# The beginning of a two-layer backbone kernel: stationary modulation weights, loads in a fixed order, modulation work held back, two norms interleaved

## The chip, the cores and the metric

The kernel runs on one core of one Trainium2 chip. The time is device microseconds (us) of one execution, the median of several runs. Engines: PE (TensorE; its weight loads are PEld), DVE (VectorE), ACT (ScalarE), POOL (GpSimd) and SP (SyncE, whose queue issues all the DMAs here). Each engine executes its own instructions in a fixed order.

## The reference

Two layers run on 1024 latent and 128 context tokens, with the same weights. Each layer is modulated by a conditioning vector, one for each group of tokens:

```python
def modulation(cond, w, b):
    m = jax.nn.silu(cond) @ w + b
    return [t[:, None, :] for t in jnp.split(m, N_MOD, axis=-1)]   # shift1, scale1, gate1, shift2, scale2, gate2

def adaln(x, g, shift, scale):
    return rms_norm(x, g) * (1.0 + scale) + shift

for l in range(DEPTH):                      # DEPTH = 2, D_MODEL = 1024
    m_ctx = modulation(c_ctx[None, :], w_mod[l], b_mod[l])
    m_lat = modulation(c, w_mod[l], b_mod[l])
    h_ctx = adaln(ctx, g_norm_mix[l], m_ctx[0], m_ctx[1])
    h_lat = adaln(lat, g_norm_mix[l], m_lat[0], m_lat[1])
    # even l: latent attention and gated MLP from h;  odd l: convolution and pooling from h
    ctx = ctx + m_ctx[2] * mix_ctx
    lat = lat + m_lat[2] * mix_lat
    # then x = x + gate2 * ConvFFN(adaln(x, ..., shift2, scale2))
```

Before anything else of layer 0 can be multiplied, `h` is needed, and for it two of the six parts ("chunks") of the first modulation: chunk 1 (scale1) and chunk 0 (shift1), each a product of a 2 x 1024 operand (two conditioning vectors) with 1024 x 1024 weights of 4 MB.

## The kernel before

Activations are held transposed: 128 channels on the partitions, 8 channel tiles (`k`, KT = 8), 1154 token columns in three blocks of 384, 384 and 386 (`BLK`). Products of the layers are made of three float32r products each (high and low halves, `mm3`), while the modulation, the transposes and the sums of squares are plain float32. In the profile a float32 product is two records, a float32r product one.

A scheduler orders each engine's instructions from the program's order and priorities; `issue_after` and `follow` add an order that it must keep. What it decides is shown further down.

The beginning of `even()` (layer 0) goes like this. `load_x(0)` loads block 0 of the input. `norm_blk` gives four steps for a block: `add(k)` squares a channel tile (ACT) and adds it up (tile `nsum`), `chain` turns the sum into the reciprocal root (tile `st` by PE, `ms` by DVE, `rs` by POOL, the diagonal `dg` by DVE, `rb` by PE), `scaled` multiplies x by it and by the scale (DVE, in place), and `shifted` adds the shift and splits the result into high (ACT, L87) and low (DVE, L88) halves of `h`. `mod_pe` makes one modulation chunk on PE: for each `k` a load of 128 x 1024 weights (`mraw`, 512 KB, from a pool of RB = 8 buffers), and two products with the two-column operand `self.sc` as the stationary side and 512 weight columns as the moving side. The two rows that result are copied (`mrow`), transposed in eight small products (`mpt`), and the bias is added (`mod`).

`even_kv` then multiplies `h` of each block by two weights: per block three tiles of 128 tokens by `wB` (`kvps`, L652 to L654, 72 records) and one product by `wA` (`qps`, L76 to L78, 24 records). `wB` comes in three units (loads `raw<-in_evB_dram`) and `wA` in one (`in_evA_dram`), each split into halves by ACT and DVE (L66, L67). After the three blocks, ten groups (`expand`) make keys and values (`kvu`, L708 to L710) from transposed, split columns (`tp` by PE, `ckvT` by ACT and DVE).

The other chunks of layer 0's modulation that are needed early (`EARLY`, chunks 2, 4 and 3) are made on DVE, by `mod_dve_steps`: 48 steps, each a load of 128 x 512 weights (256 KB, two buffers) and two instructions that accumulate into `macc` (L154 for the first step of a half, else L157). They are taken one by one from the list `self.fill` at fixed places of the program (`drip`), two per `expand`, with a lower priority, so the scheduler may also put them earlier, where it holds DVE to be idle.

`FASTB` names the blocks whose sum of squares is added up on DVE alone; for the others POOL adds pairs.

Of the kernel before, what the change touches and what calls it, by code (L numbers as in the profile page):

```python
# [19 lines left out]
P = 128  # L20
# [23 lines left out]
class Net:  # L44
# [8 lines left out]

    def unit(self, src, n=1024, gain=None, pool=None):

        nc = self.nc
        raw = self.wraw.tile([P, 1024], F32, tag="raw", name=self.nm("raw"))
        nc.sync.dma_start(out=raw[:, :n], in_=src)
# [21 lines left out]
    def split(self, hi, lo, src, shift=None):  # L80
        nc = self.nc
        if shift is None:
            ins = nc.scalar.activation(hi, src, AF.Copy)  # L83
            nc.vector.tensor_tensor(out=lo, in0=src, in1=hi.bitcast(F32), op=ALU.subtract)  # L84
            return ins
        else:
            nc.scalar.activation(hi, src, AF.Identity, bias=shift)  # L87
            nc.vector.scalar_tensor_tensor(out=lo, in0=src, scalar=shift, in1=hi.bitcast(F32),  # L88
                                           op0=ALU.add, op1=ALU.subtract)


# [25 lines left out]

    def mod_pe(self, l, ch, pool, tag, rpool):

        nc = self.nc  # L120
        ps = [self.gp.tile([P, 512], F32, tag="gp", name=self.nm("mps")) for _ in range(2)]
        for k in range(KT):
            raw = rpool.tile([P, 1024], F32, tag="mraw", name=self.nm("mraw"))
            last = nc.sync.dma_start(out=raw, in_=self.ap["wmod"][l, k * P:(k + 1) * P, ch * D:(ch + 1) * D])
            for j in range(2):
                nc.tensor.matmul(ps[j][:2, :], self.sc[:, k, :], raw[:, j * 512:(j + 1) * 512],  # L126
                                 start=(k == 0), stop=(k == KT - 1))
        pt = self.sm.tile([P, 512], F32, tag="sm", name=self.nm("mpt"))
        for j in range(2):
            row = pool.tile([2, 512], F32, tag=tag, name=self.nm("mrow"))  # L130
            nc.vector.tensor_copy(row, ps[j][:2, :])
            for m in range(4):
                i = 2 * (j * 4 + m)
                nc.tensor.transpose(pt[:, i:i + 2], row[:, m * P:(m + 1) * P], self.ident[:2, :2])
        nc.vector.tensor_tensor(
            out=self.mod[l][:, ch * 8:(ch + 1) * 8, :], in0=pt[:, :16].rearrange("p (m c) -> p m c", c=2),
            in1=self.bmod[:, l, ch * 8:(ch + 1) * 8].unsqueeze(2).to_broadcast([P, 8, 2]), op=ALU.add)
        return last

    def mod_dve_steps(self, l, ch, pool, folded):  # L140
# [4 lines left out]
        def step(h, k):  # L145
            raw = pool.tile([P, 512], F32, tag=f"mraw{k % 2}", name=self.nm("mraw"))
            c0 = ch * D + h * 512
            nc.sync.dma_start(out=raw, in_=self.ap["wmod"][l, k * P:(k + 1) * P, c0:c0 + 512])
            if k == 0:
                acc[h] = pool.tile([P, 2, 512], F32, tag=f"macc{h if folded else 0}", name=self.nm("macc"))  # L150
            a = acc[h]
            for c in range(2):
                if k == 0:
                    nc.vector.tensor_scalar(out=a[:, c, :], in0=raw, scalar1=self.sc[:, k, c:c + 1], scalar2=None,  # L154
                                            op0=ALU.mult)
                else:
                    nc.vector.scalar_tensor_tensor(out=a[:, c, :], in0=raw, scalar=self.sc[:, k, c:c + 1],  # L157
                                                   in1=a[:, c, :], op0=ALU.mult, op1=ALU.add)
# [132 lines left out]
    def norm_blk(self, x, l, w, b, hb, pool, big=None, inplace=False):  # L291
# [25 lines left out]
        def shift(src, k, o, m, c):  # L317
            so = 0 if w == 0 else 24
            self.split(hb[:, 0, k, o:o + m], hb[:, 1, k, o:o + m], src, self.mod[l][:, so + k, c:c + 1])

# [6 lines left out]

        def scaled():
            for k in range(KT):
# [3 lines left out]
        def shifted():  # L333
            for k in range(KT):
                for (o, m, ro, c) in segs:
                    shift(x[:, k, c0 + o:c0 + o + m], k, o, m, c)

# [121 lines left out]
    def even(self):  # L459
# [5 lines left out]
        with ExitStack() as e1:  # L465
            hb = self.new_hb()
            with ExitStack() as e0:
                npool = e0.enter_context(tc.tile_pool(name="en", bufs=2, reuse_waits="tile"))
                rpool = e0.enter_context(tc.tile_pool(name="er", bufs=RB, reuse_waits="tile"))
                x0 = self.xpool.tile([P, KT, T], F32, tag="x", name="x0")  # L470

                def load_x(b):
                    c0, n = BLK[b]
                    nc.sync.dma_start(out=x0[:, :, c0:c0 + n], in_=ap["xt"][:, :, c0:c0 + n])
# [12 lines left out]
                last = self.mod_pe(0, 0, npool, "mrow", rpool)  # L487
                shifted()
                with tc.issue_after(last.ins):
                    load_x(1)  # L490
                    load_x(2)
                for b in (1, 2):
                    add, chain, scaled, shifted = norm(b)
                    for k in range(KT):
                        add(k)
                    chain()
                    scaled()
                    shifted()
# [118 lines left out]

    def even_kv(self, hb, kd, vd, cw, w1, w2, w3):

# [17 lines left out]

        wB = [self.unit(ap["evB"][:, s * 288:(s + n) * 288], n * 288) for s, n in ((0, 3), (3, 3), (6, 2))]
        wA = self.unit(ap["evA"][0])
        qc0 = c1.tile([P, 2, T], F32R, name="qc0")  # L640
# [636 lines left out]
    def run(self):  # L1277
        nc, tc, ap = self.nc, self.tc, self.ap
        self.open, self.fill = {}, []
        with ExitStack() as es:  # L1280
# [62 lines left out]
NS = 3  # L1343
FASTB = (1, 2)
PRF2 = 60
# [106 lines left out]
```

## Time and profile before

| what | value |
|---|---|
| time, median of 3 runs | 2801.76 us (2801.47 to 2802.89) |
| the profiled execution | 2798.91 us, its span 2797.1 us |
| PE busy | 2702.6 us, 97% of the span |
| DVE, ACT, POOL busy | 1889.4, 1010.8 and 375.6 us |
| first 45 us: PE busy, DMA | 32.58 us, 360 GB/s |
| 45 to 75 us: PE busy, DMA, mean granted TensorE clock | 21.83 us, 105 GB/s, 0.79 |

Each row of a timeline has the start, the length, the engine, the line, the operation, output<-inputs, the shapes and a count of merged instructions, and behind them how long the engine was idle and what ended that. A row of a table by stretch has the stretch, its length, busy time (and number of records) of PE, PEld, DVE, ACT and POOL, the granted TensorE clock (1.00 is full, 0.50 half), the DMA engines' busy share and the GB/s that they moved.

### The profile page before, as it was taken

The numbers are of one execution on the slowest core, as the hardware profiler recorded it, in microseconds if no ns is written. First come the engines' busy times: TensorE is split into PE (matmuls) and PEld (weight loads), VectorE is DVE, ScalarE is ACT, GpSimd is POOL, SyncE is SP. The second block draws the span as 40 slices with busy tenths as digits, with TensorE's granted clock in tenths as the row PEclk, the third lists the DMA queues.
The fourth block names the chain that finished last, engine by engine and source line by source line (L and its number), as shares of the span: only waits on it lengthen the run. The fifth ranks groups of instructions, "written<-read, shape, count | busy, mean of one in ns | idle before, by whom it ended". The sixth has DMA issues, their size and how long they took to land.

```text
span 2797.1 us, 38522 instructions
## 1 busy us (share of the span) xinstructions
PE 2702.6 (97%) x15444; PEld 2622.6 (94%) x15444; DVE 1889.4 (68%) x3120; ACT 1010.8 (36%) x1798; POOL 375.6 (13%) x433
## 2 busy tenths in 40 slices
PE   7999989999999999999999999989999999999999
PEld 3897978889999999999999999888999999999999
DVE  5873799998787788855453878887555455554445
ACT  3543278882343222222223331225422222222331
POOL 2354155540200010000000200002000000000000
PEclk9999999999999999999999999999999999999999
DMA  7254210007143444311111011011011111111111
GB/s 277 71 154 112 86 32 23 25 1 234 53 128 114 131 133 128 119 48 46 38 46 38 10 46 39 27 39 38 31 38 46 38 46 39 45 37 40 46 46 68
DMA packets 92851, 192.64 MB, mean 69 GB/s; under 512 B 9472, under 2 KB 43136, under 8 KB 92672
## 3 DMA queue, kind: packets, MB, share of 16 engines
q1 hardware_dynamic: 92672, 190.18, 21.3%
q8 instruction: 122, 2.00, 0.3%
q14 instruction: 57, 0.47, 0.1%
HBM read 170.20 MB, written 19.95 MB: 68 GB/s over the span
## 4 chain that ended last, share of the span: by engine, by line
PE 83%; DVE 10%; DMA 3%; ACT 2%; issue 1%; POOL 1%; SPq 0%; DVEq 0%; POOLq 0%; ACTq 0%
PE fps L76 13%; PE fps L77 13%; PE fps L78 13%; PE ops L76 8%; PE ops L78 8%; PE ops L77 8%; PE av L982 2%; DMA mraw<-in_wmod_dram 2%; PE ptp L971 1%; DVE macc L157 1%; PE ips L76 1%; PE ips L77 1%; PE ips L78 1%; PE Sa L995 1%; PE mps L126 1%
## 5 line engine op out<-in xcount | busy, mean ns | idle before, releaser
L76 PE MATMUL fps<-h,wt 128*128 128x384 f32 (+1 forms) x2112 | 711.8, 339 | 1.6 <-ACT z L401 1.2
L77 PE MATMUL fps<-h,wt 128*128 128x384 f32 (+1 forms) x2112 | 713.0, 338 | 0.0
L78 PE MATMUL fps<-h,wt 128*128 128x384 f32 (+1 forms) x2112 | 712.7, 338 | 0.0
L379 DVE SCALAR_TENSOR_TENSOR x<-ops,mod,x 128x384 f32<-128x384 f32 (+1 forms) x832 | 395.6, 513 | 235.3 <-PE ops L78 233.8
L67 DVE TENSOR_TENSOR wt<-raw,wt 128x1024 fp32r<-128x1024 f32 (+2 forms) x177 | 216.8, 1235 | 385.1 <-ACT wt L66 384.6
L77 PEld LDWEIGHTS fps<-h,wt 128*128 128x128 f32 x2112 | 398.6, 189 | 0.3
L76 PEld LDWEIGHTS fps<-h,wt 128*128 128x128 f32 x2112 | 396.2, 188 | 2.5 <-ACT z L401 1.5
L78 PEld LDWEIGHTS fps<-h,wt 128*128 128x128 f32 x2112 | 398.1, 189 | 0.0
L78 PE MATMUL ops<-act,wt 128*128 128x384 f32 (+1 forms) x1056 | 358.2, 339 | 0.0
L77 PE MATMUL ops<-act,wt 128*128 128x384 f32 (+1 forms) x1056 | 357.0, 338 | 0.0
L76 PE MATMUL ops<-act,wt 128*128 128x384 f32 (+1 forms) x1056 | 355.4, 339 | 0.0
L401 ACT ACTIVATE z<-fps 128x384 f32<-128x384 f32 (+1 forms) x264 | 129.0, 493 | 602.9 <-PE fps L78 602.6
L66 ACT ACTIVATE wt<-raw 128x1024 fp32r<-128x1024 f32 (+2 forms) x177 | 182.8, 1047 | 440.1 <-PE ops L78 316.2
L157 DVE SCALAR_TENSOR_TENSOR macc<-mraw,sc,macc 128x512 f32<-128x512 f32 x280 | 214.5, 796 | 42.1 <-DMA mraw<-in_wmod_dram 41.7
L76 PEld LDWEIGHTS ops<-act,wt 128*128 128x128 f32 x1056 | 199.6, 189 | 0.0
L77 PEld LDWEIGHTS ops<-act,wt 128*128 128x128 f32 x1056 | 198.7, 188 | 0.0
L78 PEld LDWEIGHTS ops<-act,wt 128*128 128x128 f32 x1056 | 198.6, 188 | 0.1
L1181 DVE SCALAR_TENSOR_TENSOR co<-cv,c_odw,co 128x1168 f32<-128x1168 f32 x92 | 133.2, 1451 | 19.1 <-ACT co L1174 18.2
L76 PE MATMUL ops<-h,wt 128*128 128x384 f32 (+1 forms) x384 | 132.7, 351 | 7.0 <-ACT h L83 5.4
L83 ACT ACTIVATE act<-c 128x1154 fp32r<-128x1154 f32 x44 | 51.5, 1171 | 227.9 <-DVE c L422 183.5
L77 PE MATMUL ops<-h,wt 128*128 128x384 f32 (+1 forms) x384 | 132.2, 344 | 0.9 <-DVE h L84 0.9
L410 DVE SCALAR_TENSOR_TENSOR c<-z,fdw,c 128x1153 f32<-128x1153 f32 x88 | 125.7, 1429 | 8.6 <-ACT c L408 7.7
(275 smaller groups left out, 4578.0 us busy)
## 6 DMA issues: line engine op xcount, KB each, us to landing
raw<-in_fin_dram SPq DMA_DIRECT2D x88, 512.0 KB, 3.6
mraw<-in_wmod_dram SPq DMA_DIRECT2D x160, 256.0 KB, 2.8
raw<-in_fout_dram SPq DMA_DIRECT2D x44, 512.0 KB, 3.5
mraw<-in_wmod_dram SPq DMA_DIRECT2D x16, 512.0 KB, 8.8
fold<-macc SPq DMA_DIRECT2D x14, 512.0 KB, 2.9
macc<-fold SPq DMA_DIRECT2D x56, 128.0 KB, 3.3
x<-in_xt_dram SPq DMA_DIRECT2D x4, 1536.0 KB, 10.3
raw<-in_odin_dram SPq DMA_DIRECT2D x12, 512.0 KB, 3.5
```

The source lines that it names most:

```text
L66: nc.scalar.activation(wt[:, 0, :n], raw[:, :n], AF.Copy)
L67: nc.vector.tensor_tensor(out=wt[:, 1, :n], in0=raw[:, :n], in1=wt[:, 0, :n].bitcast(F32), op=ALU.subtract)
L76: mm(out, wh, ah, start=start, stop=False)
L77: mm(out, wh, al, start=False, stop=False)
L78: mm(out, wl, ah, start=False, stop=stop)
L83: ins = nc.scalar.activation(hi, src, AF.Copy)
L157: nc.vector.scalar_tensor_tensor(out=a[:, c, :], in0=raw, scalar=self.sc[:, k, c:c + 1], in1=a[:, c, :], op0=ALU.mult, op1=ALU.add)
L379: nc.vector.scalar_tensor_tensor(out=xs, in0=ps[:, o:o + w], scalar=self.mod[l][:, gch * 8 + m, c:c + 1], in1=xs, op0=ALU.mult, op1=ALU.add)
L401: nc.scalar.activation(z[:, c0:c0 + n], ps[:, :n], AF.Copy)
L410: nc.vector.scalar_tensor_tensor(out=c[:, 1:T], in0=z[:, 0:T - 1], scalar=w[:, l, ti, 0:1], in1=c[:, 1:T], op0=ALU.mult, op1=ALU.add)
L982: nc.tensor.matmul(av[:, :256].rearrange("p (j t) -> p j t", j=2), V[:, kt, h, :], rhs, start=(kt == 0 and part == 0), stop=(kt == 8 and p ...
L1181: nc.vector.scalar_tensor_tensor(out=o, in0=cv[:, j:j + COW], scalar=dw[:, j:j + 1], in1=o, op0=ALU.mult, op1=ALU.add)
```

## The change

`mod_pe` takes the weights as the stationary side and the two conditioning columns as the moving side, in 64 products of 128 x 128 weights by two columns for each chunk, in pairs of `k`; the result comes out transposed, as four partial sums that one DVE reduction adds. All the loads of the beginning go through `load_in_turn`, which keeps them in the order of the program. Chunk 1 is loaded ahead of the input. The units `wB` and `wA` are loaded inside the same order, between and behind the weights of chunk 0. For the first loads of the modulation on DVE a dependence is added on the last `h` of block 2 (`self.gate`). For blocks 1 and 2 scaling and shifting go tile by tile. Block 0 joins `FASTB`.

```diff
-    def mod_pe(self, l, ch, pool, tag, rpool):
+    def mod_pe(self, l, ch, rpool, between=()):
-        ps = [self.gp.tile([P, 512], F32, tag="gp", name=self.nm("mps")) for _ in range(2)]
+        pt = self.sm.tile([P, 512], F32, tag="sm", name=self.nm("mps"))
+        raws = []
         for k in range(KT):
+            for f in dict(between).get(k, ()):
+                f()
             raw = rpool.tile([P, 1024], F32, tag="mraw", name=self.nm("mraw"))
-            last = nc.sync.dma_start(out=raw, in_=self.ap["wmod"][l, k * P:(k + 1) * P, ch * D:(ch + 1) * D])
-            for j in range(2):
-                nc.tensor.matmul(ps[j][:2, :], self.sc[:, k, :], raw[:, j * 512:(j + 1) * 512],
-                                 start=(k == 0), stop=(k == KT - 1))
...
+            self.load_in_turn(raw, self.ap["wmod"][l, k * P:(k + 1) * P, ch * D:(ch + 1) * D])
+            raws.append(raw)
+            if k % 2:
+                for m in range(8):
+                    i = (k // 2 * 8 + m) * 2
+                    for j in (k - 1, k):
+                        nc.tensor.matmul(pt[:, i:i + 2], raws[j][:, m * P:(m + 1) * P], self.sc[:, j, :], start=(j < k), stop=(j == k))
+        mod = self.mod[l][:, ch * 8:(ch + 1) * 8, :]
+        nc.vector.tensor_reduce(out=mod, in_=pt[:, :64].rearrange("p (r m c) -> p m c r", r=4, c=2), axis=AX.X, op=ALU.add)
...
+    def load_in_turn(self, dst, src):
+
+        if self.turn:
+            with self.tc.issue_after(self.turn.ins):
+                self.turn = self.nc.sync.dma_start(out=dst, in_=src)
...
     def mod_dve_steps(self, l, ch, pool, folded):
...
-            nc.sync.dma_start(out=raw, in_=self.ap["wmod"][l, k * P:(k + 1) * P, c0:c0 + 512])
+            ld = nc.sync.dma_start(out=raw, in_=self.ap["wmod"][l, k * P:(k + 1) * P, c0:c0 + 512])
+            if self.gate:
+                self.follow(ld, self.gate, "the first norm goes before")
+                self.gate = None if k else self.gate
...
-                load_x(0)
+                self.mod_pe(0, 1, rpool, {4: [lambda: load_x(0)]}.items())
                 add, chain, scaled, shifted = norm(0)
                 for k in range(KT):
                     add(k)
-                self.mod_pe(0, 1, npool, "mrow", rpool)
                 chain()
                 self.mod_scale(0, 0)
                 scaled()
-                last = self.mod_pe(0, 0, npool, "mrow", rpool)
+                self.mod_pe(0, 0, rpool, {4: [lambda: load_w(0)], 6: [lambda: load_w(1)]}.items())
+                load_w(2)
+                load_x(1)
+                wA = self.unit(ap["evA"][0], turn=True)
+                load_x(2)
                 shifted()
...
                 for b in (1, 2):
...
-                    scaled()
-                    shifted()
+                    for k in range(KT):
+                        scaled([k])
+                        self.gate = shifted([k])
...
-FASTB = (1, 2)
+FASTB = (0, 1, 2)
```

What the scheduler makes of it on three queues. Names carry the tile's number; `x4` is a count.

PE at the end of the modulation, before: `mps` are the two rows of chunk 0, `mpt` their transposes, `rb` the block 0 factor, `kvps` the first product with `h` of block 0 (`h_5`).

```order
L286 MATMUL rb_203<-dg_204,ones 128x384
L126 MATMUL mps_216<-mraw_238,sc 2x512
L126 MATMUL mps_217<-mraw_238,sc 2x512
L126 MATMUL mps_216<-mraw_242,sc 2x512
L126 MATMUL mps_217<-mraw_242,sc 2x512
L126 MATMUL mps_216<-mraw_246,sc 2x512
L126 MATMUL mps_217<-mraw_246,sc 2x512
L134 MATMUL mpt_250<-ident,mrow_251 128x2 x4
L134 MATMUL mpt_250<-ident,mrow_257 128x2 x4
L652 MATMUL kvps_494<-wt_472,h_5_112 128x288
```

PE in the changed kernel between chunk 1 (its last two products), the factor of block 0 and chunk 0 (its first):

```order
L135 MATMUL mps_122<-sc,mraw_184 128x2
L135 MATMUL mps_122<-sc,mraw_186 128x2
L289 MATMUL st_229<-ones,nsum_206 128x1 x3
L298 MATMUL rb_237<-dg_238,ones 128x384
L135 MATMUL mps_250<-sc,mraw_251 128x2
L135 MATMUL mps_250<-sc,mraw_253 128x2
```

Before, PE had done ten of the sixteen wide products of chunk 0 ahead of `rb`; now all 64 narrow ones of chunk 0 stand behind `rb`, which waits for the chain of block 0, and behind them follow `st` of block 1 and the first `kvps`.

DVE ahead of the first `expand` in the changed kernel, behind the last `h` of block 2 (`kvred`, `kvms`, `kvst` and `qc` work on the products, `macc` is the held back modulation, `ckvT` is what `kvu` needs):

```order
L169 SCALAR_TENSOR_TENSOR macc_1016<-mraw_1101,sc,macc_1016 128x512 x2
L677 TENSOR_REDUCE kvred_828<-kvsq_915 128x1
L678 TENSOR_REDUCE kvred_828<-kvsq_915 128x1
L169 SCALAR_TENSOR_TENSOR macc_1016<-mraw_1152,sc,macc_1016 128x512 x2
L84 TENSOR_TENSOR qc_559<-qps_937,qc_559 128x386
L682 TENSOR_SCALAR kvms_920<-kvred_828 128x3
L685 TENSOR_SCALAR kvst_919<-kvred_828 128x3
L717 TENSOR_TENSOR ckvT_978<-tp_975,ckvT_978 128x256
L717 TENSOR_TENSOR ckvT_984<-tp_981,ckvT_984 128x256
```

DVE at the same place before (`h_7` is `h` of block 2):

```order
L88 SCALAR_TENSOR_TENSOR h_7_114<-x_121,mod_97,h_7_114 128x128
L659 TENSOR_REDUCE kvred_626<-kvsq_683 128x1
L84 TENSOR_TENSOR qc_490<-qps_730,qc_490 128x384
L658 TENSOR_REDUCE kvred_626<-kvsq_713 128x1
L659 TENSOR_REDUCE kvred_626<-kvsq_713 128x1
L698 TENSOR_TENSOR ckvT_909<-tp_906,ckvT_909 128x256
L698 TENSOR_TENSOR ckvT_915<-tp_912,ckvT_915 128x256
```

Sixteen `macc` instructions (eight steps) that before stood between the instructions of blocks 0 and 1 now stand behind `h_7`, fourteen of them ahead of the first `ckvT` and two behind it; at the first `kred` of the `expand` groups both kernels have done sixteen.

SP, the first loads before:

```order
L474 DMA x_121<-in_xt_dram 128x8x384
L124 DMA mraw_149<-in_wmod_dram 128x1024
L124 DMA mraw_153<-in_wmod_dram 128x1024
L124 DMA mraw_157<-in_wmod_dram 128x1024
L124 DMA mraw_161<-in_wmod_dram 128x1024
```

SP, the first loads in the changed kernel:

```order
L147 DMA mraw_123<-in_wmod_dram 128x1024
L145 DMA mraw_125<-in_wmod_dram 128x1024
L145 DMA mraw_143<-in_wmod_dram 128x1024
L145 DMA mraw_145<-in_wmod_dram 128x1024
L145 DMA x_121<-in_xt_dram 128x8x384
```

The input of block 0 moved behind four weight loads. In both kernels four small loads (`ct`, `bmod`, `gnorm`, `fdw`, together 0.25 MB) go first.

More of the change, by code (lines that the diff above doesn't have):

```diff
@@ L51, in nm, with unit @@
         return f"{s}_{self.n}"
-    def unit(self, src, n=1024, gain=None, pool=None):
+    def unit(self, src, n=1024, gain=None, pool=None, turn=False):
         nc = self.nc
         raw = self.wraw.tile([P, 1024], F32, tag="raw", name=self.nm("raw"))
-        nc.sync.dma_start(out=raw[:, :n], in_=src)
+        (self.load_in_turn if turn else nc.sync.dma_start)(raw[:, :n], src)
         wt = (pool or self.wsp).tile([P, 2, 1024], F32R, tag="wt", name=self.nm("wt"))
@@ L86, in split @@
         else:
-            nc.scalar.activation(hi, src, AF.Identity, bias=shift)
+            ins = nc.scalar.activation(hi, src, AF.Identity, bias=shift)
             nc.vector.scalar_tensor_tensor(out=lo, in0=src, scalar=shift, in1=hi.bitcast(F32),
                                            op0=ALU.add, op1=ALU.subtract)
+            return ins
     def consts(self, pool):
@@ L115, in consts @@
         nc.sync.dma_start(out=self.fdw, in_=ap["fdw"])
-    def mod_pe(self, l, ch, pool, tag, rpool):
+    def mod_pe(self, l, ch, rpool, between=()):
         nc = self.nc
-        ps = [self.gp.tile([P, 512], F32, tag="gp", name=self.nm("mps")) for _ in range(2)]
+        pt = self.sm.tile([P, 512], F32, tag="sm", name=self.nm("mps"))
+        raws = []
         for k in range(KT):
+            for f in dict(between).get(k, ()):
+                f()
             raw = rpool.tile([P, 1024], F32, tag="mraw", name=self.nm("mraw"))
-            last = nc.sync.dma_start(out=raw, in_=self.ap["wmod"][l, k * P:(k + 1) * P, ch * D:(ch + 1) * D])
-            for j in range(2):
-                nc.tensor.matmul(ps[j][:2, :], self.sc[:, k, :], raw[:, j * 512:(j + 1) * 512],
-                                 start=(k == 0), stop=(k == KT - 1))
[L128 to L138, printed above, removed]
@@ L140, in mod_dve_steps @@
+        nc.vector.tensor_tensor(out=mod, in0=mod, in1=self.bmod[:, l, ch * 8:(ch + 1) * 8].unsqueeze(2).to_broadcast([P, 8, 2]),
+                                op=ALU.add)
+    def load_in_turn(self, dst, src):
+        if self.turn:
+            with self.tc.issue_after(self.turn.ins):
+                self.turn = self.nc.sync.dma_start(out=dst, in_=src)
+        else:
+            self.turn = self.nc.sync.dma_start(out=dst, in_=src)
     def mod_dve_steps(self, l, ch, pool, folded):
@@ L318, in shift @@
             so = 0 if w == 0 else 24
-            self.split(hb[:, 0, k, o:o + m], hb[:, 1, k, o:o + m], src, self.mod[l][:, so + k, c:c + 1])
+            return self.split(hb[:, 0, k, o:o + m], hb[:, 1, k, o:o + m], src, self.mod[l][:, so + k, c:c + 1])
         def rest():
@@ L326, in rest, with scaled, shifted @@
                     shift(t, k, o, m, c)
-        def scaled():
-            for k in range(KT):
+        def scaled(ks=range(KT)):
+            for k in ks:
                 for (o, m, ro, c) in segs:
                     scale(x[:, k, c0 + o:c0 + o + m], k, o, m, ro, c)
-        def shifted():
-            for k in range(KT):
+        def shifted(ks=range(KT)):
+            for k in ks:
                 for (o, m, ro, c) in segs:
-                    shift(x[:, k, c0 + o:c0 + o + m], k, o, m, c)
+                    ins = shift(x[:, k, c0 + o:c0 + o + m], k, o, m, c)
+            return ins
         return (lambda k: add(x[:, k, c0:c0 + n]), chain) + ((scaled, shifted) if inplace else (rest,))
@@ L636, in even_kv @@
         nc.vector.memset(cst[:, 1:2], float(QD ** -0.5))
-        wB = [self.unit(ap["evB"][:, s * 288:(s + n) * 288], n * 288) for s, n in ((0, 3), (3, 3), (6, 2))]
-        wA = self.unit(ap["evA"][0])
         qc0 = c1.tile([P, 2, T], F32R, name="qc0")
@@ L1278, in run @@
         nc, tc, ap = self.nc, self.tc, self.ap
-        self.open, self.fill = {}, []
+        self.open, self.fill, self.gate = {}, [], None
         with ExitStack() as es:
```

14 lines of the change are left out of this document (8 added, 6 removed).

## The prediction

> **What bounds the kernel now.** I read the page first, then the PE timeline of the first 110 us, and then the table by stretch for the clock.
>
> ```profile
> PE 2702.6 (97%) x15444; PEld 2622.6 (94%) x15444; DVE 1889.4 (68%) x3120; ACT 1010.8 (36%) x1798; POOL 375.6 (13%) x433
> PE 83%; DVE 10%; DMA 3%; ACT 2%; issue 1%; POOL 1%; SPq 0%; DVEq 0%; POOLq 0%; ACTq 0%
> ```
>
> PE is 97% busy and 83% of the chain that ended last. So what PE loses or gains in the beginning is passed on to the end, unless a later wait takes it up. From the first `expand` on both kernels hold nearly the same order, so I count the time up to the first `kvu` and move the rest.
>
> ```profile
> 11.15 19.02 PE L126 MATMUL mps<-mraw,sc 128*2 128x512 f32 x40 [11.15 <-DMA mraw<-in_wmod_dram]
> 30.44 0.83 PE L277 MATMUL st<-ones,nsum 128*128 128x1 f32 x6
> 36.77 0.91 PE L286 MATMUL rb<-dg,ones 128*128 128x384 f32 x2
> 37.62 5.31 PE L126 MATMUL mps<-mraw,sc 128*2 128x512 f32 x12
> 43.79 0.41 PE L134 MATMUL mpt<-ident,mrow 2*128 2x2 f32 x4 [0.86 <-DVE mrow L131]
> 45.71 0.61 PE L652 MATMUL kvps<-wt,h 128*128 128x288 f32 x1 [0.91 <-ACT h L87]
> 49.84 0.29 PE L654 MATMUL kvps<-wt,h 128*128 128x288 f32 x1
> 57.38 0.34 PE L77 MATMUL qps<-h,wt 128*128 128x384 f32 x1
> 60.89 0.72 PE L277 MATMUL st<-ones,nsum 128*128 128x1 f32 x6
> 67.30 1.62 PE L286 MATMUL rb<-dg,ones 128*128 128x384 f32 x2 [5.69 <-DVE dg L284]
> 68.71 1.28 PE L277 MATMUL st<-ones,nsum 128*128 128x1 f32 x6
> 70.28 0.61 PE L652 MATMUL kvps<-wt,h 128*128 128x288 f32 x1 [0.28 <-ACT h L87]
> 73.90 0.61 PE L654 MATMUL kvps<-wt,h 128*128 128x288 f32 x1 [1.50 <-DVE h L88]
> 104.13 0.63 PE L708 MATMUL kvu<-wt,ckvT 128*128 128x512 f32 x2
> ```
>
> The reader sees two stages. From 11.15 to 43 us PE is at the modulation almost without a gap, so PE and not the loads ends that stage. From 45.71 to 104.13 (58.4 us) it multiplies three blocks, and waits 5.69, 0.28 and 1.50 us ahead of block 1.
>
> **The clock** decides what the narrow products cost.
>
> ```profile
> 292.36 1.84 PE L177 MATMUL mps<-ones,macc 128*128 128x1 f32 x16
> 294.07 0.42 PE L76 MATMUL ups<-h,wt 128*128 128x384 f32 x1
> 45.31:48.72 3.41, 3.01 (x12) 3.01 (x13) 3.31 (x8) 3.41 (x8) 0.00 (x0) 0.50 0.98 336
> 48.72:52.13 3.41, 3.41 (x27) 3.41 (x26) 3.41 (x6) 1.73 (x4) 1.89 (x2) 1.00 0.50 159
> 707.49:710.91 3.42, 3.42 (x14) 3.42 (x14) 1.53 (x4) 1.05 (x2) 1.83 (x2) 0.50 0.00 0
> 710.91:714.32 3.41, 3.41 (x12) 3.41 (x11) 0.62 (x1) 0.52 (x1) 1.00 (x1) 0.50 0.00 0
> 707.30 1.30 PE L277 MATMUL st<-ones,nsum 128*128 128x1 f32 x6 [2.21 <-DVE nsum L269]
> 708.46 0.67 PE L76 MATMUL ops<-h,wt 128*128 128x384 f32 x1
> 41.89:45.31 3.42, 1.85 (x11) 0.72 (x9) 2.93 (x7) 0.47 (x2) 0.00 (x0) 1.00 1.06 384
> L126 PE MATMUL mps<-mraw,sc x4: 1013/1058/1061, 11.2 to 13.7; 128*2 128x512 f32 x4
> ```
>
> A product with a 128 x 128 float32 stationary side and one moving column is paced by its weight load: 16 records in 294.07 - 292.36 = 1.71 us, 0.107 each, at full clock; six in 1.28 us at 68.71, 0.213 each, at half clock. The granted clock changes on a grid of 3.41 us. The stretch from 45.31 was at half clock with PE busy for 3.01 us, all wide products, and the next was at full. The stretch from 707.49 was at half clock with PE busy for all 3.42 us, and the next was still at half. It differs in its first 0.97 us, which were `st` products with one moving column; the wide ones began at 708.46 and filled 72%. [...] The new modulation consists of such products, 128 records a chunk, each moving two columns, and the first four records of before (1013 to 1061 ns against 592 later) show that the kernel starts at half clock. So I take half clock for the whole modulation.
>
> [...]
>
> **The change part by part.** *Order of loads.* DMA is the limit of the first pair:
>
> ```profile
> 0.00:5.00 5.00, 0.00 (x0) 0.00 (x0) 0.23 (x3) 1.50 (x2) 1.05 (x11) 1.00 0.36 66
> 5.00:10.00 5.00, 0.00 (x0) 0.00 (x0) 0.00 (x0) 0.24 (x1) 0.00 (x0) 1.00 1.05 390
> ```
>
> 0.33 MB are there at 5 us, then 0.39 MB each us. Before, small loads, block 0 and one `mraw` (0.25 + 1.57 + 0.52 MB) are through at 10.2, and PE began at 11.15. Now 0.25 + 1.05 MB are through at 7.5: PE begins at 8.5, 2.7 us earlier. The later loads keep ahead of a PE at half clock (a buffer comes free with each pair, every 6.8 us, and 1 MB takes 2.6 us), so the fixed order gives no more, and PE doesn't come to wait for loads.
>
> *Stationary weights.* Before, 64 records of 0.43 us (5.31 / 12 less the tail), 27.4 us for both chunks, and the copies and transposes. Now 64 products, 128 records, for each chunk: 128 x 0.213 = 27.3 us a chunk. Chunk 1 ends at 35.8. Then `st` 1.28, and the chain to `rb`, which PE now waits for with nothing beside it:
>
> ```profile
> 32.45 0.56 DVE L284 TENSOR_TENSOR dg<-ident,rs 128x384 f32<-128x384 f32 x1 [0.43 <-POOL rs L583]
> 44.83 0.17 DVE L135 TENSOR_TENSOR mod<-mpt,bmod 128x16 f32<-128x16 f32 x1 [0.49 <-PE mpt L134]
> ```
>
> `st` ended at 31.27 and `dg` at 33.01, so 1.7 us; `rb` at half clock takes 1.4 (67.30 to 68.71). That is 40.2. Chunk 0: 40.2 + 27.3 = 67.5. `st` of block 1 takes PE to 68.8; reduction, bias and `h` (0.88 us from the add at 44.83 to 45.71, and 0.2 for the reduction) are done by then. First `kvps` at 68.8, before 45.71: **+23.1**. Ends: +21.5 if the clock opens for one stretch, +24.5 if pairs wait for semaphores.
>
> *The blocks.* Loads, squares and sums of blocks 1 and 2 are long done at 68.8, and the 16 `macc` are out of the way. With `h` of a block ready tile by tile, DVE needs 8 x 0.54 to scale and 8 x 0.54 to shift, under 9 us of a block's 13.7 on PE, so I let the waits ahead of block 1 vanish; POOL is out of block 0's sums, which now lie beside chunk 1. PE work: 57 `kvps` in 57.38 - 49.84 (0.132 each), 20 `qps` in 60.89 - 57.38 (0.176), so a block is 72 x 0.132 + 24 x 0.176 = 13.7 us; three are 41.2; two `rb` and an `st` 2.5; half clock until one or two stretches are filled with wide products loses 1.7 to 3.4, say 2.3. Sum 46.0, against 58.4: **-12.4**. Ends: -13 (one stretch) and 0 (all of the waits come back). The blocks end at 114.8.
>
> *The held back modulation.* Before, sixteen `macc` lay under blocks 0 and 1:
>
> ```profile
> L157 DVE SCALAR_TENSOR_TENSOR macc<-mraw,sc,macc 128x512 f32<-128x512 f32 x14 | 11.8, 869 | 0.0
> 82.00 5.29 DVE L314 SCALAR_TENSOR_TENSOR x<-x,scl,rb 128x256 f32<-128x256 f32 x16 [3.98 <-PE rb L286]
> 99.59 2.36 DVE L67 TENSOR_TENSOR wt<-raw,wt 128x1024 fp32r<-128x1024 f32 x2 [0.43 <-ACT wt L66]
> 126.05 0.87 DVE L154 TENSOR_SCALAR macc<-mraw,sc 128x512 f32<-128x512 f32 x2
> 126.95 2.67 DMA mraw<-in_wmod_dram
> 127.18 1.40 DVE L157 SCALAR_TENSOR_TENSOR macc<-mraw,sc,macc 128x512 f32<-128x512 f32 x2
> 96.25 0.74 DVE L698 TENSOR_TENSOR ckvT<-tp,ckvT 128x256 fp32r<-128x256 f32 x2
> 107.82 0.68 DVE L716 TENSOR_REDUCE kred<-ksq 128x8 f32<-128x512 f32 x1
> ```
>
> Now fourteen stand in DVE's queue between `h` of block 2 and `ckvT`, and PE waits for `ckvT`. `rb` of block 2 is done at 89, scaling 5.3 and shifting 5.3 with some small ones 1.5 bring DVE to 101. Then 0.8 + 6 x 1.33 for `macc`, 2.3 for the splits, 3.2 for `kvred`, `qc` and small ones, 0.7 for `ckvT`, and about a microsecond of waits for loads (two buffers, 2.67 us a load): 117. PE has eight `kvu` records (1.8 us) that need only ACT's half, so it stands as if it had begun at 115.4, **+0.6** more; SP's queue holds `evA` behind these loads, needed only later. DVE reaches the first `kred` at 121.5 (two splits, two `macc`) against 107.82, 13.7 later, which PE may or may not feel. Ends +10.7 (DVE hidden) and +13.7; I take the middle, **+12.2 us** in all. The profiled execution is 2798.91, 2.85 below the median 2801.76; on the median the sum is 2814.0.
>
> **The rivals.** *1, faster: the clock opens early in the modulation.* For it: PE is busy without a gap, and wide products with only two stationary columns did open the clock at 14.6. [...] Against: the stretch from 707.49. Two stretches (6.8 us) at half clock give 32 records, the other 96 take 10.3: chunk 1 ends at 25.6, `rb` at 29, chunk 0 at 42.7, `kvps` begin at 43.6 (-2.1); the blocks then take 43.7 (-14.7), and DVE's queue gives back 2: about -15, 2787.
>
> *2, slower still: the blocks wait for DVE as before.* DVE's waits ahead of block 1 return if its rows for blocks 1 and 2 stand too late; from 9 us for a block's scaling and shifting against 13.7 I think not. With none of the 12.4 regained +23.1, 2825.
>
> *3, no change: the clock opens for chunk 0 alone,* by `st` and `rb`. Chunk 0 then takes 13.7 instead of 27.3, and the blocks begin warm: 12.2 - 13.6 - 2.3 and what DVE gives back, -2, 2800. Against: `rb` is 1.3 us of a stretch of 3.4.
>
> **How the numbers follow.** Forecast 0.80 (2807.5 to 2821), rival 1 0.11, rival 2 0.05, rival 3 0.04. A measurement here can tell 0.2% (5.6 us) from no change. Slower by more than that: 0.80 and 0.05, less 0.01 for a forecast that comes out small: 0.84; within 0.05; faster 0.11. The range goes from 2804, where a little of rival 3 and a small forecast end, to 2824, near rival 2; rival 1 is left out.
>
> **What would show it.** Right: about 256 narrow L135 records 0.213 apart at granted clock 0.50, first `kvps` near 69, no PE wait over 1 us ahead of block 1, first `kvu` near 115 to 117, then equal stages. Wrong: spacing 0.107 and `kvps` near 44 (the clock); waits for `h` within the blocks (rival 2); a first `kvu` as late as 120 (DVE's backlog).

## The result, and the profile after

The changed kernel took 2821.98 us (median of four executions, 2814.34 to 2822.44), the kernel before beside it 2802.32: a ratio of 1.0068, 95% interval 1.0056 to 1.0080. That is slower by 19 to 20 us, inside the range and with the sign that was forecast, 8 us above the predicted time. The profiled execution is the quickest of the four, 2814.34 with a span of 2812.6, so its rows show 15.5 us more than the span before and not 19 to 20.

The page, busy times and the chain that ended last:

```profile
PE 2727.6 (97%) x15620; PEld 2672.9 (95%) x15620; DVE 1892.2 (67%) x3122; ACT 1010.0 (36%) x1798; POOL 371.1 (13%) x429
PE 83%; DVE 9%; DMA 3%; ACT 2%; POOL 1%; issue 1%; SPq 0%; DVEq 0%; POOLq 0%; ACTq 0%
```

The shares are nearly those of before. PE is busy 25 us longer, 22.4 of them up to the last `kvu` (147.3 us there, before 124.9). The timeline of PE shows where:

```profile
7.17 0.56 PE L135 MATMUL mps<-sc,mraw 128*128 128x2 f32 x2 [7.17 <-DMA mraw<-in_wmod_dram]
9.45 27.04 PE L135 MATMUL mps<-sc,mraw 128*128 128x2 f32 x126 [1.72 <-DMA mraw<-in_wmod_dram]
36.35 1.42 PE L289 MATMUL st<-ones,nsum 128*128 128x1 f32 x6
39.91 1.62 PE L298 MATMUL rb<-dg,ones 128*128 128x384 f32 x2 [2.13 <-DVE dg L296]
41.32 27.31 PE L135 MATMUL mps<-sc,mraw 128*128 128x2 f32 x128
69.80 0.61 PE L671 MATMUL kvps<-wt,h 128*128 128x288 f32 x1
73.65 0.44 PE L672 MATMUL kvps<-wt,h 128*128 128x288 f32 x1
74.74 0.29 PE L673 MATMUL kvps<-wt,h 128*128 128x288 f32 x1
116.31 0.50 PE L727 MATMUL kvu<-wt,ckvT 128*128 128x512 f32 x1 [0.42 <-ACT ckvT L716]
121.25 0.50 PE L729 MATMUL kvu<-wt,ckvT 128*128 128x512 f32 x1 [2.58 <-DVE ckvT L717]
122.62 0.63 PE L727 MATMUL kvu<-wt,ckvT 128*128 128x512 f32 x1
126.16 0.40 PE L727 MATMUL kvu<-wt,ckvT 128*128 128x512 f32 x1
271.99 1.06 PE L1029 MATMUL Sc<-ctx,ctx 96*128 96x128 f32 x8
645.61 0.52 PE L76 MATMUL ops<-h,wt 128*128 128x384 f32 x1
```

Read it by the lags behind the kernel before. The first `kvps` stands at 69.80 against 45.71, +24.1. From 74.5 on the records are short (0.29 in place of 0.44): the clock opened there, for the first time. The first `kvu` stands at 116.31 against 104.13, +12.2. Then PE waits 2.58 us for the low half of `ckvT`, and at the 31st `kvu` record (111.5 before, 128.7 now) the lag is 17.2 us. Part of it comes back before the attention. For that the same two rows of the kernel before, the first context scores and the first output product:

```profile
257.88 1.05 PE L1010 MATMUL Sc<-ctx,ctx 96*128 96x128 f32 x8
629.22 0.34 PE L76 MATMUL ops<-h,wt 128*128 128x384 f32 x1
```

The lag is 14.1 at the scores, 16.4 at the output product and 15.5 at the end.

What DVE does ahead of the wait at 121.25 (its timeline, changed kernel):

```profile
103.78 0.87 DVE L166 TENSOR_SCALAR macc<-mraw,sc 128x512 f32<-128x512 f32 x2
112.12 2.80 DVE L169 SCALAR_TENSOR_TENSOR macc<-mraw,sc,macc 128x512 f32<-128x512 f32 x2 [0.60 <-DMA mraw<-in_wmod_dram]
118.86 1.40 DVE L169 SCALAR_TENSOR_TENSOR macc<-mraw,sc,macc 128x512 f32<-128x512 f32 x2
120.78 0.74 DVE L717 TENSOR_TENSOR ckvT<-tp,ckvT 128x256 fp32r<-128x256 f32 x2
```

From 103.78 to 120.3 the fourteen held back `macc` take 11.0 us of DVE's time, with the splits and `kvred` between them, and `ckvT` comes behind them.

### The profile page after: what moved, and what is told of

Its sections match the earlier page's. It is cut to its first block, busy times and chain, and to the rows that moved or that the text cites. A ratio compares the mean times of both kernels' runs of the same rounds, so it can differ in the third digit from the quotient of the medians.

```text
span 2812.6 us, 38880 instructions
## 1 busy us (share of the span) xinstructions
PE 2727.6 (97%) x15620; PEld 2672.9 (95%) x15620; DVE 1892.2 (67%) x3122; ACT 1010.0 (36%) x1798; POOL 371.1 (13%) x429
## 4 chain that ended last, share of the span: by engine, by line
PE 83%; DVE 9%; DMA 3%; ACT 2%; POOL 1%; issue 1%; SPq 0%; DVEq 0%; POOLq 0%; ACTq 0%
PE fps L76 13%; PE fps L77 13%; PE fps L78 13%; PE ops L76 8%; PE ops L77 8%; PE ops L78 8%; PE av L1001 2%; DMA mraw<-in_wmod_dram 2%; PE mps L135 2%; PE ptp L990 1%; PE ips L77 1%; PE ips L76 1%; PE ips L78 1%; DVE macc L169 1%; DVE h L88 1%
```

## The experiments

Each median stands beside that of the kernel before on the same chip. The ratios are of all executions and need not be the quotients of the two medians. "First kvps" and "first kvu" are read from the PE timeline of one profiled execution.

| kernel | median us | before | ratio, 95% interval | first kvps | first kvu |
|---|---|---|---|---|---|
| changed, again | 2818.97 | 2800.75 | 1.0068 (1.0056 to 1.0081) | 69.62 | 116.27 |
| 128 moving columns | 2806.78 | 2800.75 | 1.0026 (1.0015 to 1.0036) | 47.60 | 98.70 |
| 64 moving columns | 2819.14 | 2801.22 | 1.0063 (1.0044 to 1.0083) | 68.94 | 114.78 |
| before with narrow products | 2819.72 | 2800.75 | 1.0071 (1.0057 to 1.0084) | 74.06 | 121.21 |
| norms not interleaved | 2816.72 | 2800.73 | 1.0055 (1.0041 to 1.0069) | 70.01 | 115.94 |
| no hold | 2818.73 | 2801.22 | 1.0059 (1.0044 to 1.0074) | 71.70 | 118.60 |
| wide products | 2803.33 | 2800.75 | 1.0009 (1.0000 to 1.0018) | 43.36 | 99.44 |
| wide, no hold | 2801.27 | 2801.22 | 0.9997 (0.9987 to 1.0007) | 43.65 | 103.94 |
| 128 columns, no hold | 2803.47 | 2801.22 | 1.0009 (1.0000 to 1.0018) | 46.88 | 104.27 |
| wide, no hold, sums on POOL | 2807.07 | 2800.73 | 1.0018 (1.0009 to 1.0027) | 44.62 | 106.53 |
| the same, modulation later | 2808.74 | 2800.73 | 1.0028 (1.0017 to 1.0038) | 43.35 | 103.56 |
| before with fill products | 2799.78 | 2800.90 | 0.9995 (0.9986 to 1.0004) | 46.67 | 103.40 |

**The changed kernel again.** No edit.

> The changed kernel once more, nothing edited. Its profiled execution took 2814.34 us, three others 2821.5 to 2822.5. If the 8 us between them is a matter of where the 3.41 us grid of the clock falls on the program, executions should again be of two kinds, about 2814 and 2822, with equal beginnings (first kvps 69.8, first kvu 116.3) and four or five more stretches at half clock in the longer kind. If instead the beginning itself differs (another first load, another first opening of the clock), the first kvu would stand some 8 us later in the longer kind.

It took 2818.03 to 2820.95, profiled 2818.03. The two kinds were not found; executions scatter. Its timeline of PE:

```profile
121.22 0.50 PE L729 MATMUL kvu<-wt,ckvT 128*128 128x512 f32 x1 [2.57 <-DVE ckvT L717]
274.39 1.13 PE L1029 MATMUL Sc<-ctx,ctx 96*128 96x128 f32 x8 [0.73 <-issue]
648.54 0.34 PE L76 MATMUL ops<-h,wt 128*128 128x384 f32 x1
```

At 121.22 the two executions agree within 0.03 us; at the scores they are 2.4 us apart, at the output product 2.9. So the beginning repeats, and what differs between executions comes behind it. There the granted clock differs, 0.99 and 0.97 from 130 to 260, as the table by stretch has it for the first and for the second execution (the granted clock is the third number from the right):

```profile
130.00:260.00 130.00, 124.56 (x718) 112.37 (x717) 85.62 (x157) 56.97 (x96) 72.71 (x70) 0.99 0.49 135
```

```profile
130.00:260.00 130.00, 123.88 (x708) 111.79 (x708) 85.72 (x157) 56.33 (x95) 72.95 (x70) 0.97 0.48 135
```

The first got through 718 records there, the second through 708. That the phase of the 3.41 us grid sets this is an estimate of the author's and was not shown: no run fixed the phase.

**How much has to move to open the clock.** The moving side gets 128 or 64 columns in place of two, the two conditioning columns over and over, accumulated over four `k`. Products and weight loads stay 64 a chunk.

```diff
-            if k % 2:
+            if k % 4 == 3:
+                pt.append([self.gp.tile([P, 512], F32, ...) for _ in range(2)])       # 64 columns: range(1)
                 for m in range(8):
...
-                        nc.tensor.matmul(pt[:, i:i + 2], raws[j][:, m * P:(m + 1) * P], self.sc[:, j, :], ...)
+                        nc.tensor.matmul(o, raws[j][:, m * P:(m + 1) * P], self.scw[:, j, :128], ...)   # or :64
```

> The changed kernel with 128 moving columns (the two conditioning columns 64 times over) in place of two, in groups of four k; as many products and weight loads as before. Theory (weight loads with almost nothing moving do not open the clock): now the clock opens within two stretches of 3.41 us, after which the records are 0.107 to 0.12 us apart; the modulation takes some 31 us in place of 54.5, the first kvps stands at 42 to 46 and not at 69.8. DVE then has more to do than PE (scaling, shifting, sums and the held back macc, some 60 us from there), so the first kvu comes at 92 to 104 and the end at 2790 to 2806. Rival (the weight load costs 0.213 us whatever moves): records stay 0.213 apart, first kvps 71, end 2816 to 2824.

> The changed kernel with 64 moving columns. If what opens the clock is the share of a 3.41 us stretch in which columns move, then at half clock 64 columns of 128 fill about half of a stretch, too little to open it (85% was enough, 72% was not): records 0.213 apart, first kvps 70 to 73, time 2816 to 2824. If any moving beyond a few columns is enough: as with 128 columns, first kvps 46 to 49, time 2805 to 2810.

The table by stretch, with 128 columns:

```profile
11.18:14.60 3.42, 3.33 (x16) 3.04 (x16) 0.00 (x0) 0.00 (x0) 0.00 (x0) 1.00 1.07 395
14.60:18.01 3.41, 3.41 (x32) 3.41 (x32) 0.88 (x3) 1.67 (x4) 0.00 (x0) 1.00 1.04 412
```

and with 64:

```profile
14.15:17.56 3.41, 3.41 (x18) 3.41 (x17) 0.71 (x2) 1.58 (x4) 0.00 (x0) 1.00 1.04 411
51.69:55.11 3.42, 3.42 (x18) 3.42 (x17) 2.73 (x5) 2.60 (x5) 0.00 (x0) 1.00 1.06 377
```

The stretches are 3.41 us long, the grid of the clock in the kernel before (half clock there from 45.31 to 48.72 and from 707.49 to 714.32, one stretch and two). With 128 columns 16 records fit in the first and 32 in the next: one stretch was enough, and the clock opened at 14.6. With 64 columns PE and its weight loads were busy for whole stretches, and after 40 us there are still some 16 records in each (18 where those cut by an edge are counted twice over): 0.213 apart, no opening before the first `kvps` (at 68.94, a little ahead of the 70 to 73 expected). (The clock's column reads 1.00 in all four rows; see the last section.) This tells the theory from its rival: with the same loads, the moving columns decided (16 to 18 records in 3.41 us with 64, 32 with 128). How large a share of a record that is can be estimated from the wide products of the kernel before, which took 0.43 us for 512 columns at full clock and 0.84 at half (the first five began from 11.15 to 14.52). By this estimate 64 columns move for some 0.105 of the 0.213 us of a record, and 128 for nearly all of it. One half was not enough here, the whole was; nothing between them was run. Nor does the kernel before show what share is enough, and the 85% of the expectation is the author's estimate: PE was busy for 3.01 of 3.41 us (88%) in the stretch from 45.31, and the next was at full clock; it was busy for 3.01 us in that from 523.17 too, with 256 and 384 moving columns, and the next was still at half.

The second thing was not foreseen in this size. With 128 columns the first `kvps` comes 22 us earlier than in the changed kernel, yet the time is only some 12 us shorter, and still longer than before. Two of the expected ranges were just missed: the first `kvps` stands at 47.60 (42 to 46 expected), and the time is 2806.78 (up to 2806). PE waits 4.23 us for `h` of block 0. The rows behind that wait:

```profile
43.84 0.52 ACT L273 ACTIVATE nsum<-x 128x384 f32<-128x384 f32 x1 [4.93 <-DMA x<-in_xt_dram]
44.81 0.56 DVE L277 TENSOR_TENSOR nsum<-nsum,nsq 128x384 f32<-128x384 f32 x1 [4.14 <-ACT nsq L273]
45.29 0.16 DVE L145 TENSOR_TENSOR mod<-mod,mps 128x8 f32<-128x8 f32 x1
```

ACT waits for the load of block 1, DVE for ACT's square, and the last addition of chunk 0, which needs neither, stands behind that sum in DVE's queue.

**Which part of the change makes the blocks short.** Three kernels. The kernel before with only `mod_pe`'s products replaced by the new ones; the changed kernel with the norms not interleaved; the changed kernel without the hold:

```diff
 (before, products only)
-                nc.tensor.matmul(ps[j][:2, :], self.sc[:, k, :], raw[:, j * 512:(j + 1) * 512], ...)
+                        nc.tensor.matmul(pt[:, i:i + 2], raws[j][:, m * P:(m + 1) * P], self.sc[:, j, :], ...)
 (changed, norms apart)
-                    for k in range(KT):
-                        scaled([k])
-                        self.gate = shifted([k])
+                    scaled()
+                    self.gate = shifted()
 (changed, no hold)
-                        self.gate = shifted([k])
+                        shifted([k])
```

> The kernel before with only the modulation's products changed to the new form; loads, hold, sums and norms as before. Theory (the blocks are quick after a late start because DVE has caught up by then, and the narrow form is what makes the start late): modulation 2 x 27.3 us from 11.15, first kvps 71 to 73, three blocks 45 to 48 us, no backlog of macc ahead of ckvT, end 2810 to 2817. Rival (the hold and the interleaving are what made the blocks 12 us shorter): blocks 55 to 58 us as before, first kvu at 128 or later, end 2824 to 2830.

> The changed kernel with the norms of blocks 1 and 2 written as before, scaling first and shifting behind it. Theory (the late start makes the blocks quick, not the interleaving): first kvps 69.8, blocks 45 to 46 us, no wait of over 1 us ahead of block 1, end as the changed kernel's, 2814 to 2821. Rival (interleaving lets PE begin block 1 earlier): waits of 2 us or more ahead of block 1, blocks 48 us or longer, end 2817 to 2825.

> The changed kernel without the dependence that holds the modulation on DVE back; the scheduler now puts sixteen macc among the sums, under the modulation on PE, where DVE is idle. Theory (the held back macc cost PE some 6 us at the kvu, where DVE is 12 us late): first kvps 69.8 as with the hold, blocks 45.5 us, no wait of 2.6 us for ckvT, groups of kvu some 5 us earlier than with the hold, end 2811 to 2816 against 2814 to 2821. Rival (the hold is what keeps the blocks short): blocks 50 us or longer, end as with the hold or later.

The PE timelines, of the kernel before with the narrow products:

```profile
74.06 0.61 PE L650 MATMUL kvps<-wt,h 128*128 128x288 f32 x1
121.21 0.50 PE L706 MATMUL kvu<-wt,ckvT 128*128 128x512 f32 x1 [1.07 <-ACT ckvT L695]
```

of the changed kernel with the norms apart:

```profile
70.01 0.61 PE L670 MATMUL kvps<-wt,h 128*128 128x288 f32 x1
115.94 0.50 PE L726 MATMUL kvu<-wt,ckvT 128*128 128x512 f32 x1 [0.42 <-ACT ckvT L715]
120.89 0.53 PE L728 MATMUL kvu<-wt,ckvT 128*128 128x512 f32 x1 [2.58 <-DVE ckvT L716]
```

and of the changed kernel without the hold:

```profile
41.81 1.62 PE L298 MATMUL rb<-dg,ones 128*128 128x384 f32 x2 [3.89 <-DVE dg L296]
71.70 0.61 PE L671 MATMUL kvps<-wt,h 128*128 128x288 f32 x1
118.60 0.50 PE L727 MATMUL kvu<-wt,ckvT 128*128 128x512 f32 x1 [1.15 <-ACT ckvT L716]
```

The first missed two of its ranges (first `kvps` 74.06, expected 71 to 73; 2819.72 us, expected up to 2817). From the first `kvps` to the first `kvu` the three take 47.2, 45.9 and 46.9 us (46.5 in the changed kernel, 58.4 before), with no wait in the blocks. The first has neither hold nor interleaving nor another `FASTB`, so the lateness of the start alone makes the blocks short, and the narrow products alone make the kernel as slow as the whole change does (1.0071 against 1.0068). Interleaving gave nothing that shows; the scheduler had mostly undone it (with and without it DVE scales all eight pieces of block 1, and 15 or 16 of the 16 of block 2, ahead of their `h`).

The hold costs at one place what it saves at another. Without it the wait of 2.58 us for DVE's `ckvT` is gone, and the lag stays at 14.6 us, from the 31st `kvu` record (126.0) to the last (162.2, before 147.6). But two `macc` now stand in DVE's queue directly ahead of `dg`:

```profile
39.60 1.41 DVE L169 SCALAR_TENSOR_TENSOR macc<-mraw,sc,macc 128x512 f32<-128x512 f32 x2
41.10 0.56 DVE L296 TENSOR_TENSOR dg<-ident,rs 128x384 f32<-128x384 f32 x1
```

so `rb` waits 3.89 us and not 2.13, and the first `kvps` is 1.9 us later. The forecast of 2811 to 2816 failed: the profiled execution was in it (2812.73), the median (2818.73) is that of the kernel with the hold, and the intervals of the two ratios overlap. Neither is shown to be better.

**What the rest of the change is worth when the modulation is quick.** The changed kernel with the products of before, with and without the hold, and 128 columns without the hold:

```diff
 (changed, wide products)
-                        nc.tensor.matmul(pt[:, i:i + 2], raws[j][:, m * P:(m + 1) * P], self.sc[:, j, :], ...)
+                nc.tensor.matmul(ps[j][:2, :], self.sc[:, k, :], raw[:, j * 512:(j + 1) * 512], ...)
+        ... (the copies mrow and transposes mpt as before the change)
```

> The changed kernel with the modulation's products as before the change (two conditioning columns stationary, 512 weight columns moving, copies and transposes), everything else of the change kept. Theory (the form of the products costs the 24 us): first PE 7 to 8.5, first kvps 42 to 46, no earlier first kvu than some 95 since DVE's queue (sums, scaling, shifting, held back macc) becomes the limit, end 2790 to 2804. Rival (the new order of loads, the hold and the interleaving cost part of it): first kvps 55 or later, end over 2810.

> The wide products of before and no hold, with the new order of loads and the interleaving. Theory (backlog): first kvps 43 to 44, first kvu 98 to 102, end 2795 to 2801. Rival (DVE is the limit in any order): end 2802 to 2805, as with the hold.

> 128 moving columns and no hold. With the hold the groups of kvu went from 4.6 us ahead of the kernel before to 2.3 us behind it. Theory (that loss is the backlog of macc, which the idle DVE of the first 45 us can take instead): first kvps 46 to 48, first kvu at 98 to 102, still ahead by 2 to 5 us at the last kvu, end 2796 to 2802, that is the time of the kernel before or a little less. Rival (DVE is the limit from the first kvps to the first kvu in any order): the blocks grow by what the kvu gain, end 2805 to 2808 as with the hold.

PE with wide products and the hold:

```profile
63.49 1.52 PE L300 MATMUL rb<-dg,ones 128*128 128x384 f32 x2 [4.85 <-DVE dg L298]
99.44 0.63 PE L730 MATMUL kvu<-wt,ckvT 128*128 128x512 f32 x2
110.98 0.47 PE L730 MATMUL kvu<-wt,ckvT 128*128 128x512 f32 x1 [2.43 <-DVE V L745]
```

and without the hold:

```profile
65.69 1.62 PE L300 MATMUL rb<-dg,ones 128*128 128x384 f32 x2 [5.12 <-DVE dg L298]
103.94 0.71 PE L730 MATMUL kvu<-wt,ckvT 128*128 128x512 f32 x2
```

The theory on the form of the products holds: the first `kvps` stands at 43.4, 2.3 us ahead of the kernel before (earlier loads), and the time is that of before. The theory on the backlog holds in part only. With the hold the first `kvu` is 4.7 us early with wide products, and waits for DVE give that away again: the last `kvu` stands at 150.2 (149.9 with 128 columns), before 147.6. Without it the first `kvu` is at 103.9 and 104.3, where it was before the change and not at 98 to 102, and the last at 148.8 and 147.8. The times without the hold, 2801.27 and 2803.47, lie between the ranges of theory and rival. Against the kernel before they are lower than with the hold (0.9997 for 1.0009, 1.0009 for 1.0026); the first pair of intervals overlaps, the second only at its ends. So the hold seems to cost a few us when the modulation is quick, but with `macc` in neither place is anything gained on the kernel before. In the blocks PE waits for `dg` of block 1 again: 4.85 and 5.12 us with wide products, 3.05 with 128 columns and no hold, 5.69 before. With 128 columns and the hold it waits for `h` of block 1 instead (0.79 and 2.46 us).

**Is it the amount of DVE's work?** Wide products without the hold, the sums of blocks 1 and 2 added in pairs on POOL; and the same with the modulation on DVE begun behind the fourth `ckvT`:

```diff
-FASTB = (0, 1, 2)
+FASTB = (0,)
 (second kernel, in the loop over expand)
+            if i == 2:
+                self.gate = self.low
-            self.drip(KVDRIP)
+            self.drip(KVDRIP if i > 1 else 0)
```

> Wide products, new order of loads, no hold, and the sums of squares of blocks 1 and 2 added in pairs on POOL (which is idle there), so DVE has eight additions of 0.56 us less to do. Theory (with the clock open early DVE is the limit from the first kvps to the first kvu): first kvps 43 to 44, first kvu 3 to 5 us earlier than without this (103.9), at 99 to 101, end 2796 to 2799. Rival (a limit other than DVE's amount of work, such as the chain of block 1 through st, POOL and rb): first kvu 103 or later, end 2800 to 2804.

> As the kernel with the sums on POOL, and the modulation on DVE begins only behind the low half of the fourth ckvT, so that none of it lies ahead of the first kvu. Theory (DVE's amount of work is the limit): DVE has some 12 us less to do ahead of the first kvu, which comes at 92 to 96; part is given back later, end 2790 to 2798. Rival (the work put off costs PE as much later, as the hold of the changed kernel did): the kvu stage loses what the blocks gained, end 2800 to 2806.

The theory failed in both, and both kernels are slower than before, by more than their rivals had it (up to 2804 and 2806). PE of the first:

```profile
64.49 1.44 PE L291 MATMUL st<-ones,nsum 128*128 128x1 f32 x6 [4.27 <-DVE nsum L283]
106.53 0.40 PE L730 MATMUL kvu<-wt,ckvT 128*128 128x512 f32 x1
```

PE now waits 4.27 us for `nsum` of block 1 ahead of `st`: adding in pairs makes the chain squares, sum, `st`, `dg`, `rb`, `h` longer, though it takes work off DVE. Taking all `macc` out of the way as well brought the first `kvu` back to 103.56 only (the time of that kernel holds too what the work put off costs later, which was not taken apart). So less work on DVE hardly shortens the wait. From 44 to 60 us DVE is busy for 15.7 of the 16 us with wide products and no hold, 13.7 with the hold and 10.2 in the last kernel, and PE's wait for `dg` is 5.12, 4.85 and 4.22 us (in the last with 1.68 us for `nsum` ahead of it). With an early start it is the chain of block 1 that ends last, and what holds it up can be read with wide products and the hold:

```profile
54.70 0.83 PE L291 MATMUL st<-ones,nsum 128*128 128x1 f32 x6
59.72 0.15 DVE L293 TENSOR_SCALAR ms<-st 128x3 f32<-128x3 f32 x1
62.60 0.73 DVE L298 TENSOR_TENSOR dg<-ident,rs 128x384 f32<-128x384 f32 x1 [0.65 <-POOL rs L607]
```

`st` ends at 55.5, and `ms`, which needs nothing else, comes at 59.72. In DVE's queue sums of block 2 and `kvred` stand ahead of it, and DVE is busy for 5.79 of the 6 us from 54 to 60. No run moved `ms` ahead of them, so it is not shown that this order is worth its 4 us.

**Do waits cost twice?** The kernel before with products that nobody reads in the wait ahead of block 1:

```diff
+            if gi == 0:
+                for i in range(30):
+                    nc.tensor.matmul(o[:, :384], wA[:, 0, :P], hb[0][:, 0, i % KT, :384], start=True, stop=True)
```

> The kernel before with 30 products added that nobody reads (128 x 128 stationary, 384 moving columns, 0.176 us each), one ahead of and 29 behind the sums of block 1, where PE waits 5.69 us for dg and after which it ran at half clock from 65.8 to 79.4. Theory (waits cost twice, since they close the clock): the clock stays open, kvps of block 1 begin at 69 to 70.3 as before but run at full clock, rb of block 2 comes some 3 us earlier, first kvu at 98 to 102 against 104.1, end 2795 to 2798.5 against 2800.7. Rival (PE waits for h of DVE instead, which is the limit): first kvu 103.5 to 105, end 2800 to 2802.

The same stretch, in the kernel before and with the fill products:

```profile
65.79:79.44 13.65, 10.36 (x37) 9.22 (x38) 11.28 (x23) 5.65 (x11) 1.93 (x2) 0.50 0.04 15
```

```profile
65.79:79.44 13.65, 10.59 (x56) 9.36 (x55) 11.98 (x25) 6.26 (x12) 2.89 (x3) 0.87 0.07 21
```

and PE there, with the fill products:

```profile
74.13 0.40 PE L654 MATMUL kvps<-wt,h 128*128 128x288 f32 x1 [2.39 <-DVE h L88]
103.40 0.63 PE L715 MATMUL kvu<-wt,ckvT 128*128 128x512 f32 x2
```

The clock was held open (0.87 for 0.50), but the quicker PE waits longer for `h` (2.39 us, before 1.50), and the first `kvu` came 0.7 us earlier, not 2 to 6 (1.7 us, counted from the first `kvps`, which was 1.0 late in this execution). The time, 2799.78 us and a ratio of 0.9995 (0.9986 to 1.0004), is no different, and lies between the two ranges. Half a clock cost little there, since PE had to wait for block 1 anyway.

## Why the prediction was right, and where it was off

- *The clock* was right, and carries the result. Chunk 0 takes 27.31 us for 128 records, 0.213 each, as forecast (27.3); the clock opened at 74.5, behind the first whole stretch of wide products (15 records in the 3.41 us from 71.16, PE busy for all of it, 25 in the next 3.42). Before the change, records with a 128 x 128 stationary side and one moving column stood 0.107 us apart at full clock (sixteen in 1.71 us) and 0.213 at half. With 64 moving columns the records stayed 0.213 apart though PE was busy for whole stretches (3.41 of 3.41 us); with 128 they went from 16 to 32 a stretch at 14.6. So in these runs moving columns, and not loads, opened the clock; which share of a stretch they have to fill, no run shows. The sign "at granted clock 0.50" could not be read, since the column has 1.00 there; the spacing stands for it.
- *The order of loads*: PE began at 7.17 and not 8.5, but then waited 1.72 us for the next weights; chunk 1 ended at 36.35 (35.8 forecast).
- *The first kvps* at 69.80 (68.8): +24.1, between the ends +21.5 and +24.5.
- *The blocks* took 46.5 us (46.0), without a wait: -11.9 for -12.4. The reason given, that loads and sums are done by then, is borne out by the kernel with the narrow products alone; the part given to tile by tile norms is not.
- *The held back modulation* is the term that was mis-sized. It was put at +0.6, as if begun at 115.4, with `ckvT` at 117 (the 1.8 us taken off 117 give 115.2 and +0.4), and the middle of the two ends has 1.5 us for it. `h` of block 2 ended at 103.7 and not 101, two of the `macc` took 2.80 us together in place of 1.40 (112.12; why stays open), and `ckvT` came at 120.78. PE waited 2.58 us, and that wait closed the clock for a stretch: `kvu` records of 0.63 at 122.62 (granted clock 0.51 from 122.31), again 0.40 at 126.16. From +12.2 at the first `kvu` the lag grew to 17. Some 3 us of it were given back later. The remark that PE "may or may not feel" DVE's 13.7 us was too mild: it felt it. The first `kvu` came inside the 115 to 117 that was to show the prediction right, but the DVE backlog that a first `kvu` at 120 was to show came all the same, eight records later. That without the hold the median is no lower shows the term as a place of the loss, not as a sum that can be saved.
- *Then equal stages* was nearly right in the profile: +14.1 at the scores, +15.5 at the end. The medians are 3 to 4 us higher still. Between the two traced executions of the changed kernel a like difference (3.6 us in the span) comes behind the beginning, where the slower one has the lower granted clock (0.97 for 0.99 from 130 to 260); for the other executions this is not shown.
- *Rival 1* (the clock opens early) did not come, and its price was wrong: with 128 columns the clock did open at 14.6, and the time was 2806.8, 2803.5 without the hold, not 2787. The working let `kvps` begin at 43.6 and the blocks take 43.7 us; they began at 47.60 and 46.88 and took 51.1 and 57.4, with PE waiting for `h` or `dg` of block 1 again. *Rivals 2 and 3* did not come: no wait in the blocks, and `rb` did not open the clock for chunk 0.
- *The number*: 2821.98 is 1 us above the 2807.5 to 2821 that the chance of 0.80 was given for, and nearer to rival 2's 2825 than to 2814.0. The trace decides for the forecast's path all the same: rival 2 needs waits ahead of block 1 and blocks of 58 us, and there were none and 46.5.

## What to carry to other kernels

Before turning a product round, so that a wide weight becomes the stationary side and only a few columns move, look at what the clock will do: here the narrow records stood 0.213 us apart to the end of the modulation, where such records took 0.107 at full clock, and the narrow products alone cost as much as the whole change (1.0071 against 1.0068). A stage that starts later gives back what its followers had been waiting for (24 us late at the start, 12 us late three blocks later), and a stage that starts earlier runs into the same wait; so price a shift by the next chain that must end, not by PE's work. Work that is held back is not gone: look for what stands behind it in its engine's queue when it is done.

## What the runs showed of the hardware

- Records with 64 moving columns did not open the clock from 8.88 to the first `kvps` at 68.94 (PE busy for 3.41 of 3.41 us in the stretches from 14.15 and 51.69; 102 records in the 21.86 us from 45.95). With 128 moving columns one stretch did (busy 3.33 of 3.42 us, 16 records), and the next held 32.
- The profile's clock column reads 1.00 in the changed kernel from the start up to 122.31, where the clock first falls, though the narrow records are 0.213 us apart and the wide ones become short only at 74.5. At the start of these programs the clock has to be read from the spacing.
- Behind a wait of 2.58 us, shorter than a stretch, the clock was at half for the next one (0.51; `kvu` 0.63 in place of 0.40 us). PE was busy for 1.06 us of the stretch that holds the wait:

```profile
118.90:122.31 3.41, 1.06 (x5) 0.89 (x6) 3.26 (x9) 1.06 (x1) 0.86 (x1) 1.00 0.90 326
122.31:125.73 3.42, 3.42 (x11) 2.64 (x10) 3.16 (x6) 2.87 (x5) 0.00 (x0) 0.51 0.49 158
```

- Adding products that nobody reads kept the clock up through a wait (0.87 for 0.50) and brought no time that shows (0.9995, 0.9986 to 1.0004); the wait behind it grew from 1.50 to 2.39 us.
